# Weight splits of 1024 columns, and nine conditioning parts summed on VectorE, in a one-core diffusion step

## The chip, the cores and the metric

One core of a Trainium2 chip runs the whole program. The metric is the device time in microseconds from start to end of one execution, lower is better. The engines are TensorE (PE, with its weight loads PEld), VectorE (DVE), ScalarE (ACT), GpSimd (POOL) and SyncE (SP), whose queue issues the weight transfers. All work on the same on-chip memory, each through its own queue, in the order in which its instructions stand there.

## The reference

Two layers over 256 tokens (128 context, 128 latent) of width 2048, in float32: layer 0 mixes attention and a recurrent scan, layer 1 is a convolution module, and each is followed by a gated ffn of width 5504. Every norm is shifted, scaled and gated by vectors computed from two conditioning vectors; this is the part that the change touches:

```python
def adaln(cvec, w, b):
    return (jax.nn.silu(cvec) @ w + b)[:, None, :]
...
    sh1p, sc1p, g1p, sh2p, sc2p, g2p = jnp.split(adaln(c_ctx[None, :], w_ada[l], b_ada[l]), 6, axis=-1)
    sh1s, sc1s, g1s, sh2s, sc2s, g2s = jnp.split(adaln(c, w_ada[l], b_ada[l]), 6, axis=-1)
    hp = rmsnorm(xp, norm_g[l, 0]) * (1.0 + sc1p) + sh1p
...
def conv_ffn(h, w_up, w_dw, w_down):
    u = dwconv(h @ w_up, w_dw)
    gate, val = jnp.split(u, 2, axis=-1)
    return (jax.nn.silu(gate) * val) @ w_down
```

w_ada has 2 x 2048 x 12288 elements, and each is used for two vectors only. All other weights are used for all 256 tokens.

## The kernel before, in words

**The gemms.** Every large product goes through `gemm` (or `gemm_joint` for the first projection). Activations lie in memory as pairs of a rounded value and its remainder (`split`, `modulated`); weights are split in the same way, into `hi` and `lo`. For each slice of 128 rows of the inner dimension (a *k-step*) and each tile of 128 output columns, three matmuls of 256 tokens are issued (L251, L253, L254): hi with the value, hi with the remainder, lo with the value. A k-step of 512 weight columns is 12 matmuls. The ffn runs an up projection of the first 22 of 43 column blocks, a down projection of these, and then the same for the other 21.

**The weight stream.** `sub_iter` walks over all plans in a fixed order and gives one load of up to 1024 columns (512 KB) into a `raw` buffer, of which there are seven, then one conversion per k-step. `emit_sub` issues the load from SP, copies the columns to `hi` on ScalarE (L194), and subtracts on VectorE, or on GpSimd in the first conv gemm and for half of the second, to get `lo` (L196). The eight slots of `wbt` each hold one k-step. `next_sub` keeps the stream six k-steps ahead of TensorE.

**The conditioning.** `ada_order` lists 30 parts; the first ten are narrow (two or four blocks of 128 columns), the other 20 have 8 blocks, 1024 columns. `ada_pe` computes a part on TensorE: silu of the two vectors, padded to 32 columns, is the stationary operand, and w_ada streams past it as four matmul calls of 256 columns per 128 rows (L429). In the late parts a step is two raw loads and eight such calls; eight steps make a part. `ada_turn` transposes the result on VectorE, and `ada_gen` adds the bias and sets the part as done. Loads for w_ada take their buffers from the same seven as the weights, in the order of the code.

**What sets the order.** The code calls `ada_step` from the `fill` functions of the gemms: every sixth k-step in both ffns (`fill0`, `fill2`, after the sixteenth), every fourth in the conv gemm (`fill1`) and in the output projection. `ada_until` runs what is left where a part is needed: g2 ahead of the down projection, sh1 of layer 1 ahead of the conv module, g1 ahead of its second gemm, sh2 behind that gemm, ahead of the second ffn. Between the two conv gemms a depthwise convolution of 31 taps ends, on VectorE and, in late groups, on TensorE (L1608). The scheduler then orders each engine's instructions by the code's order and its own estimate of times; the raw buffers rotate.

## Time and profile before

| | |
|---|---|
| median of 3 runs | 2783.12 us (2778.12 to 2791.07) |
| the profiled execution | 2783.63 us, span 2781.1 us |
| mean granted TensorE clock | 0.977 |
| raw<-in_w_ada | 384 loads, 512 KB each, median 5.5 us to landing |
| matmul instructions L429 on w_ada | 3840 in 1920 calls, between 13.8 and 2215.0 us |

By time from the start of the span: the first projection, up to about 260 us, with the narrow parts beside it; the recurrent scan and attention up to about 750 us; the output projection; the first ffn from about 840 to 1640 us; the first conv gemm to 1890, the second from 1915 to 2009; the second ffn to the end.

A row of the windows gives a stretch in us, then busy us and number of instructions of PE, PEld, DVE, ACT and POOL, the granted clock, the busy share of the DMA engines and what they moved in GB/s. A row of groups gives line, engine, operation, what is written from what, count, busy us and mean length in ns, then the idle time before them and what ended it. Rows of the timeline and of the chain of waits begin with start and length in us. Matmuls overlap, so that time per matmul is read from a stretch and its count, not from its length.

### The profile page before, as it was taken

Reading aid. Unit: us, or ns where it says so; the run is one execution under the profiler, and the core shown is the slowest. Engines: PE = TensorE matmul, PEld = TensorE weight load, DVE = VectorE, ACT = ScalarE, POOL = GpSimd, SP = SyncE. Lnnn points to the kernel's source line nnn. Section 1 sums busy time; section 2 is a strip of 40 time slices with the busy share of each in tenths; the row PEclk is TensorE's granted clock in tenths of the full one; section 3 lists DMA queues with packets and bytes.
Section 4 is the critical chain, followed back from the end, with each engine's and each line's share of the span. In section 5 each row is a group of like instructions: output and inputs, shape, how many; then the busy total and the mean of one; then the engine's idle time right before and its main releaser. Section 6 shows DMA issues by size and latency. Waiting matters only on the chain.

```text
span 2781.1 us, 64420 instructions
## 1 busy us (share of the span) xinstructions
PE 2709.5 (97%) x25355; PEld 2496.1 (90%) x25355; DVE 1777.3 (64%) x3873; ACT 1404.9 (51%) x2866; POOL 321.7 (12%) x409
## 2 busy tenths in 40 slices
PE   6999998999999999999999999999999999999998
PEld 5899995767999999999999988988999999999998
DVE  3568757666568656546656558997476665566665
ACT  4336644545446545434555455447565554455554
POOL 2000011111100000000000017765300000000000
PEclk9999999989899999999999999999999999999999
DMA  9996657656276887788788767883568865565563
GB/s 295 327 281 215 178 154 258 219 165 220 94 232 208 267 257 250 259 263 252 250 267 261 261 204 257 289 251 107 182 207 254 268 189 189 185 189 183 174 199 113
DMA packets 446991, 616.83 MB, mean 222 GB/s; under 512 B 33461, under 2 KB 317464, under 8 KB 446048
## 3 DMA queue, kind: packets, MB, share of 16 engines
q1 hardware_dynamic: 442288, 600.83, 68.4%
q0 software_dynamic: 3040, 6.57, 0.7%
q10 hardware_dynamic: 1360, 5.33, 0.5%
q8 instruction: 198, 3.24, 0.5%
q14 instruction: 105, 0.86, 0.1%
HBM read 604.75 MB, written 7.86 MB: 220 GB/s over the span
## 4 chain that ended last, share of the span: by engine, by line
PE 94%; DMA 2%; DVE 2%; ACT 1%; issue 0%; SPq 0%; DVEq 0%; ACTq 0%
PE mm L251 24%; PE mm L254 23%; PE mm L253 23%; PE ada L429 7%; DMA raw<-in_w_ada 2%; PE mm L1050 2%; PE mm L303 1%; PE mm L304 1%; PE mm L305 1%; PE mm L1608 1%; PE mm L288 1%; PE mm L1083 1%; DVE hbt L550 1%; PE mm L290 1%; DMA raw<-in_w_in 1%; PE mm L291 1%
## 5 line engine op out<-in xcount | busy, mean ns | idle before, releaser
L194 ACT ACTIVATE wbt<-raw 128x512 fp32r<-128x512 f32 (+2 forms) x1560 | 945.4, 612 | 1073.7 <-PE mm L253 803.9
L196 DVE TENSOR_TENSOR wbt<-raw,wbt 128x512 fp32r<-128x512 f32 (+2 forms) x1384 | 922.6, 672 | 732.0 <-ACT wbt L194 708.1
L251 PE MATMUL mm<-hbt,wbt 128*128 128x256 f32 x3888 | 1102.6, 285 | 5.5 <-ACT hbt L548 3.5
L253 PE MATMUL mm<-hbt,wbt 128*128 128x256 f32 x3888 | 1089.6, 281 | 4.3 <-DVE hbt L550 4.3
L254 PE MATMUL mm<-hbt,wbt 128*128 128x256 f32 x3888 | 1088.6, 280 | 0.0
L251 PEld LDWEIGHTS mm<-hbt,wbt 128*128 128x128 f32 x3888 | 732.2, 189 | 44.6 <-ACT wbt L194 20.2
L253 PEld LDWEIGHTS mm<-hbt,wbt 128*128 128x128 f32 x3888 | 731.9, 188 | 9.1 <-DVE hbt L550 7.1
L254 PEld LDWEIGHTS mm<-hbt,wbt 128*128 128x128 f32 x3888 | 734.5, 189 | 1.0 <-issue 0.4
L251 PE MATMUL mm<-u,wbt 128*128 128x256 f32 x1344 | 378.5, 282 | 0.0
L253 PE MATMUL mm<-u,wbt 128*128 128x256 f32 x1344 | 375.0, 279 | 0.0
L254 PE MATMUL mm<-u,wbt 128*128 128x256 f32 x1344 | 375.0, 279 | 0.0
L196 POOL TENSOR_TENSOR wbt<-raw,wbt 128x512 fp32r<-128x512 f32 (+1 forms) x176 | 215.4, 1234 | 961.9 <-ACT wbt L194 946.1
L251 PEld LDWEIGHTS mm<-u,wbt 128*128 128x128 f32 x1344 | 252.2, 188 | 8.6 <-ACT wbt L194 7.4
L429 PE MATMUL ada<-raw,silu_c 128*32 128x256 f32 (+2 forms) x3840 | 238.3, 347 | 20.9 <-DVE ht L545 8.4
L254 PEld LDWEIGHTS mm<-u,wbt 128*128 128x128 f32 x1344 | 252.7, 188 | 0.0
L253 PEld LDWEIGHTS mm<-u,wbt 128*128 128x128 f32 x1344 | 251.4, 187 | 0.0
L429 PEld LDWEIGHTS ada<-raw,silu_c 128*32 128x32 f32 x3840 | 99.3, 110 | 95.2 <-issue 18.9
L1615 DVE SCALAR_TENSOR_TENSOR cu<-mm,vec,cu 128x256 f32<-128x256 f32 x428 | 174.6, 471 | 2.8 <-ACT cu L1599 1.2
L1504 DVE SCALAR_TENSOR_TENSOR cv<-mm,vec,cv 128x254 f32<-128x254 f32 x344 | 148.1, 474 | 14.1 <-ACT cv L1499 14.0
L303 PE MATMUL mm<-hbt,wbt 128*128 128x256 f32 x304 | 90.4, 298 | 0.4 <-ACT hbt L548 0.3
L304 PE MATMUL mm<-hbt,wbt 128*128 128x256 f32 x304 | 85.7, 282 | 0.0
L305 PE MATMUL mm<-hbt,wbt 128*128 128x256 f32 x304 | 85.0, 280 | 0.0
(443 smaller groups left out, 2772.4 us busy)
## 6 DMA issues: line engine op xcount, KB each, us to landing
raw<-in_w_ada SPq DMA_DIRECT2D x384, 512.0 KB, 5.5
raw<-in_w_up SPq DMA_DIRECT2D x688, 256.0 KB, 3.7
raw<-in_w_down SPq DMA_DIRECT2D x168, 512.0 KB, 4.6
raw<-in_w_pw SPq DMA_DIRECT2D x128, 256.0 KB, 5.0
raw<-in_w_in SPq DMA_DIRECT2D x128, 192.0 KB, 5.8
raw<-in_w_in SPq DMA_DIRECT2D x48, 512.0 KB, 3.9
raw<-in_w_out SPq DMA_DIRECT2D x32, 512.0 KB, 4.5
raw<-in_w_pw SPq DMA_DIRECT2D x32, 512.0 KB, 4.5
```

The costliest lines, as they stand in the source:

```text
L194: act.activation(w[:, 0, 0:n], src, AF.Copy)
L196: pl.lo(pl.count).tensor_tensor(out=w[:, 1, 0:n], in0=src, in1=w[:, 0, 0:n].bitcast(F32), op=ALU.subtract)
L251: pe.matmul(ps, lhsT=hi, rhs=r[:, 0:TT], start=(ki == 0 and (nl > 0 or j % 2 == 0)), stop=False, skip_group_check=True)
L253: pe.matmul(ps, lhsT=hi, rhs=r[:, TT:2 * TT], start=False, stop=False, skip_group_check=True)
L254: pe.matmul(ps, lhsT=lo, rhs=r[:, 0:TT], start=False, stop=(ki == nk - 1), skip_group_check=True)
L303: pe.matmul(ps, lhsT=hi, rhs=r[:, 0:TT], start=(i == 0), stop=False, skip_group_check=True)
L304: pe.matmul(ps, lhsT=hi, rhs=r[:, TT:2 * TT], start=False, stop=False, skip_group_check=True)
L305: pe.matmul(ps, lhsT=lo, rhs=r[:, 0:TT], start=False, stop=(i == len(rw) - 1), skip_group_check=True)
L429: pe.matmul(ps[32 * j:32 * j + 32, 0:nb * 32], lhsT=silu_c[:, kt, :], rhs=rv[:, j], start=(kt == 0), stop=(kt == KT - 1))
L1050: pe.matmul(dst_[h][:, s * TT:(s + 1) * TT], lhsT=src[pr, s], rhs=kr[pr, s].rearrange("p a t -> p (a t)"), start=True, stop=True)
L1504: dve.scalar_tensor_tensor(out=o[:, :, a_], in0=v2(ps)[:, :, b_], scalar=w(k, ct), in1=o[:, :, a_], op0=ALU.mult, op1=ALU.add)
L1615: dve.scalar_tensor_tensor(out=o, in0=pads[a](k), scalar=V("w_dw", k * KT + ct), in1=o, op0=ALU.mult, op1=ALU.add)
```

## The change

It has three parts. The weight split works on a whole load: `emit_load` issues the load, one ScalarE copy and one subtract of up to 1024 columns, and `wbt` has four slots of 1024 columns, each given back when all its k-steps were used. Nine conditioning parts (`AS_VEC`) are no longer multiplied on TensorE: `ada_vec` multiplies each load of w_ada by the silu value of its row (a scalar per partition) and adds it to an accumulator `av`, once per vector, on VectorE; what is left, a sum over 128 partitions, is made by eight matmul calls with a selector `sel`, four per vector. And the fills call `ada_step` every second k-step in both ffns, in the first one only until part (1, g1, 0) is done. A part in `ada_vec` has 38 steps, where one of `ada_pe` had ten.

```diff
-    WB = 8
-    LA = WB - 2
+    WB = 4
+    LA = 6
...
-        wbt[0] = wbp.tile([P, WB, 2, 512], F32R, tag="wb", name="wbt")
+        wbt[0] = wbp.tile([P, WB, 2, 1024], F32R, tag="wb", name="wbt")
...
+        if len(ends) >= WB and ends[-WB] > free[0]:
             return False
...
+        w = wbt[0][:, len(ends) % WB]
+        act.activation(w[:, 0, 0:na * n], v, AF.Copy)
+        pl.count += 1
+        pl.lo(pl.count).tensor_tensor(out=w[:, 1, 0:na * n], in0=v, in1=w[:, 0, 0:na * n].bitcast(F32),
+                                      op=ALU.subtract)
+        subs.extend(w[:, :, a * n:(a + 1) * n] for a in range(na))
+        ends.append(len(subs))
...
+    AS_VEC = [(l, nm, i) for l, nm in ((0, "g2"), (1, "sc1"), (1, "sh1"), (1, "g2")) for i in range(2)] + [(1, "g1", 0)]
...
+    def ada_vec(l, nm, b0, nb):
...
+        nxt = load(0)
+        yield
+        for kt in range(KT):
+            raw, nxt = nxt, (load(kt + 1) if kt < KT - 1 else None)
+            for s in range(2):
+                sc = silu_c[:, kt, s:s + 1]
+                if kt == 0:
+                    dve.tensor_scalar(out=av[:, s], in0=raw, scalar1=sc, scalar2=None, op0=ALU.mult)
+                else:
+                    dve.scalar_tensor_tensor(out=av[:, s], in0=raw, scalar=sc, in1=av[:, s], op0=ALU.mult, op1=ALU.add)
+                yield
+        for _ in range(3):
+            yield
+        ps = psa.tile([P, 256], F32, tag="ada", name="ada")
+        for s in range(2):
+            rv = av[:, s].rearrange("p (b j c) -> p j b c", j=4, c=32)
+            for j in range(4):
+                pe.matmul(ps[32 * j:32 * j + 32, 0:nb * 32], lhsT=sel[:, s], rhs=rv[:, j], start=(s == 0), stop=(s == 1))
+        yield
+        return ada_turn(ps, nb)
...
-            tr = yield from ada_pe(l, nm, b0, nb, 2 if l or nm == "g2" else 1)
+            if (l, nm, part) in AS_VEC:
+                tr = yield from ada_vec(l, nm, b0, nb)
+            else:
+                tr = yield from ada_pe(l, nm, b0, nb, 2 if l else 1)
...
-                if cnt[0] % 6 == 0 and cnt[0] > 16:
+                if cnt[0] % 2 == 0 and cnt[0] > 16 and (1, "g1", 0) not in ada_done:
                     ada_step()
...
-                if cnt[0] % 6 == 0 and cnt[0] > 16:
+                if cnt[0] % 2 == 0 and cnt[0] > 16:
                     ada_step()
```

The parts that stay on TensorE after the first ffn are the second of g1 and all of sc2 and sh2 of layer 1. Their steps still run in `fill1` and, what is left, at the `ada_until` calls behind it. On the SP queue, from the end of the first conv gemm to the second ffn (`in_w_pw` are the conv weights, 128x2x512 those of the second gemm; `in_w_up` those of the ffn), there stood before:

```order
L566 DMA raw<-in_w_pw 128x4x128 x2
L410 DMA raw<-in_w_ada 128x1024 x2
L566 DMA raw<-in_w_pw 128x4x128 x6
L566 DMA raw<-in_w_pw 128x2x512 x32
L569 DMA raw<-in_w_up 128x2x256 x24
L410 DMA raw<-in_w_ada 128x1024 x2
```

and in the changed kernel:

```order
L603 DMA raw<-in_w_pw 128x2x512
L412 DMA raw<-in_w_ada 128x1024 x2
L603 DMA raw<-in_w_pw 128x2x512 x2
L412 DMA raw<-in_w_ada 128x1024 x10
L603 DMA raw<-in_w_pw 128x2x512 x29
L606 DMA raw<-in_w_up 128x2x256 x4
L412 DMA raw<-in_w_ada 128x1024 x30
L606 DMA raw<-in_w_up 128x2x256 x20
L444 DMA raw<-in_w_ada 128x1024
```

Ten loads of w_ada now stand ahead of the fourth load of the second conv gemm, and 30 behind the first two loads (four k-steps) of the ffn. On TensorE, at the end of the second conv gemm (L267 to L269 are its last matmuls, `ones` and `dg` the norm's), there stood before:

```order
L267 MATMUL mm<-hbt,wbt 128x256
L268 MATMUL mm<-hbt,wbt 128x256
L269 MATMUL mm<-hbt,wbt 128x256
L491 MATMUL mm<-ones,acc 128x2
L491 MATMUL mm<-ones,sq 128x2
L491 MATMUL mm<-ones,acc 128x2
L491 MATMUL mm<-ones,sq 128x2
L506 MATMUL mm<-dg,ones 128x256
L251 MATMUL mm<-hbt,wbt 128x256 x2
```

and in the changed kernel:

```order
L270 MATMUL mm<-hbt,wbt 128x256
L431 MATMUL ada<-raw,silu_c 32x256 x28
L528 MATMUL mm<-ones,acc 128x2
L528 MATMUL mm<-ones,sq 128x2
L528 MATMUL mm<-ones,acc 128x2
L528 MATMUL mm<-ones,sq 128x2
L431 MATMUL ada<-raw,silu_c 32x256 x8
L543 MATMUL mm<-dg,ones 128x256
L431 MATMUL ada<-raw,silu_c 32x256 x24
L252 MATMUL mm<-hbt,wbt 128x256 x2
L431 MATMUL ada<-raw,silu_c 32x256 x4
```

The calls on 16 loads of w_ada stand between the conv gemm and the third matmul of the ffn, and those on 14 more (not shown) among its first four k-steps and ahead of the fifth. On VectorE, in the second up projection of the first ffn (L196 and L194 are conversions, L1504 and L1544 the ffn's taps, L1512, L1519, L1552 and L1559 its products and splits, L456 the new sums), a piece of the queue before:

```order
L1504 SCALAR_TENSOR_TENSOR cv<-mm,vec,cv 128x2x127 x2
L196 TENSOR_TENSOR wbt<-raw,wbt 128x512
L1504 SCALAR_TENSOR_TENSOR cv<-mm,vec,cv 128x2x127 x4
L196 TENSOR_TENSOR wbt<-raw,wbt 128x512
L1504 SCALAR_TENSOR_TENSOR cv<-mm,vec,cv 128x2x127
L196 TENSOR_TENSOR wbt<-raw,wbt 128x512
L1504 SCALAR_TENSOR_TENSOR cv<-mm,vec,cv 128x2x127
L1512 TENSOR_TENSOR cv<-cv 128x256
L196 TENSOR_TENSOR wbt<-raw,wbt 128x512
```

and in the changed kernel:

```order
L1544 SCALAR_TENSOR_TENSOR cv<-mm,vec,cv 128x2x127 x2
L456 SCALAR_TENSOR_TENSOR av<-raw,silu_c,av 128x1024 x2
L194 TENSOR_TENSOR wbt<-raw,wbt 128x1024
L1544 SCALAR_TENSOR_TENSOR cv<-mm,vec,cv 128x2x127 x2
L194 TENSOR_TENSOR wbt<-raw,wbt 128x1024
L456 SCALAR_TENSOR_TENSOR av<-raw,silu_c,av 128x1024 x2
L194 TENSOR_TENSOR wbt<-raw,wbt 128x1024
L1552 TENSOR_TENSOR cv<-cv 128x256 x2
L194 TENSOR_TENSOR wbt<-raw,wbt 128x1024 x2
```

A pair of sums of 1024 columns now stands between conversions of 1024, and the conversions behind it on the queue come after it.

More of the change, by code (lines that the diff above doesn't have):

```diff
@@ L154, in __init__ @@
             self.count = 0
-    stream = {"slot": 0, "stop": None}
+    stream = {"stop": None}
     def sub_iter():
@@ L164, in sub_iter, with emit_load @@
                     na = min(1024 // g['n'], len(kts) - i)
-                    yield ("load", pl, g, kts[i], na)
-                    for a in range(na):
-                        yield ("conv", pl, g, kts[i], a)
+                    yield pl, g, kts[i], na
                     i += na
     subs = []
+    ends = []
+    used = [0]
+    free = [0]
     stream_it = [None]
-    def emit_sub():
+    def emit_load():
         if stream['stop'] is not None and len(subs) >= stream['stop']:
+            return False
+        if len(ends) >= WB and ends[-WB] > free[0]:
             return False
@@ L177, in emit_sub, with next_sub @@
             stream_it[0] = sub_iter()
-        while True:
-            ev = next(stream_it[0], None)
-            if ev is None:
-                return False
-            kind, pl, g, kt, a = ev
-            n = g["n"]
-            if kind == "load":
-                raw = rawp.tile([P, 1024], F32, tag="raw", name="raw")
-                v = raw[:, 0:a * n]
-                pl.view(sp, v, g, kt, a)
-                stream["raw"] = v
-                continue
-            raw = stream["raw"]
-            w = wbt[0][:, stream["slot"] % WB]
-            stream["slot"] += 1
-            src = raw[:, a * n:(a + 1) * n]
-            act.activation(w[:, 0, 0:n], src, AF.Copy)
-            pl.count += 1
-            pl.lo(pl.count).tensor_tensor(out=w[:, 1, 0:n], in0=src, in1=w[:, 0, 0:n].bitcast(F32), op=ALU.subtract)
-            subs.append(w)
-            return True
+        ev = next(stream_it[0], None)
+        if ev is None:
+            return False
+        pl, g, kt, na = ev
+        n = g["n"]
+        raw = rawp.tile([P, 1024], F32, tag="raw", name="raw")
+        v = raw[:, 0:na * n]
+        pl.view(sp, v, g, kt, na)
+        w = wbt[0][:, len(ends) % WB]
[5 more added lines that the diff above has]
+        ends.append(len(subs))
+        return True
     def prefetch(n=LA):
         while len(subs) < used[0] + n:
-            if not emit_sub():
+            if not emit_load():
                 break
-    used = [0]
-    def next_sub(la=LA):
+    def next_sub(la=LA, held=False):
+        if not held:
+            free[0] = used[0]
         prefetch(1 + la)
@@ L432, in ada_pe, with load @@
         return ada_turn(ps, nb)
+    def ada_vec(l, nm, b0, nb):
+        nw = nb * P
+        c0 = SEG[nm] * D + b0 * P
+        av = nrm_[0].tile([P, 2, 1024], F32, tag="av", name="av", bufs=1)
+        def load(kt):
+            raw = rawp.tile([P, 1024], F32, tag="raw", name="raw")
+            sp.dma_start(out=raw, in_=A["w_ada"][l, kt * P:(kt + 1) * P, c0:c0 + nw])
+            return raw
+        nxt = load(0)
[18 more added lines that the diff above has]
+        return ada_turn(ps, nb)
     def ada_turn(ps, nb):
@@ L1429, in tile_step @@
         dve.memset(silu_c, 0.0)
+        dve.memset(sel, 0.0)
+        for s in range(2):
+            dve.memset(sel[:, s, s:s + 1], 1.0)
         nrm_[0] = nrm0_scope.enter_context(scoped("nrm0", 2, "right"))
```

5 lines of the change are left out of this document (3 added, 2 removed).

## The prediction

> **What bounds the kernel now.** I read the page first, for the busy shares and the chain that ended last.
>
> ```profile
> span 2781.1 us, 64420 instructions
> PE 2709.5 (97%) x25355; PEld 2496.1 (90%) x25355; DVE 1777.3 (64%) x3873; ACT 1404.9 (51%) x2866; POOL 321.7 (12%) x409
> ...
> PE 94%; DMA 2%; DVE 2%; ACT 1%; issue 0%; SPq 0%; DVEq 0%; ACTq 0%
> ```
>
> TensorE holds 94% of the chain, so TensorE time removed in a dense stretch is time gained. Next, windows: one in the first ffn, with conditioning work, and one in the second, behind it (busy us, with instructions in brackets, for PE, PEld, DVE, ACT, POOL; then granted clock, DMA share, GB/s).
>
> ```profile
> 980.00:1050.00 70.00, 70.00 (x632) 65.69 (x631) 43.20 (x81) 36.37 (x69) 0.00 (x0) 1.00 0.79 251
> 2450.00:2520.00 70.00, 70.00 (x597) 70.00 (x595) 46.32 (x86) 39.70 (x74) 0.00 (x0) 1.00 0.62 189
> ```
>
> TensorE never pauses in either. Without conditioning work 597 matmuls take 70 us, 0.1173 us each; a k-step (512 weight columns, 12 matmuls) takes 1.41 us. VectorE is busy for 43 to 46 of 70 us: it has some 25 us to give, no more. The chain of waits shows what a conditioning step on TensorE costs (start, length):
>
> ```profile
> 998.73 1.00 PE ada L429 x16
> ...
> 1008.41 1.00 PE ada L429 x16
> ```
>
> One such step (two loads, eight matmul calls, each two instructions) comes every six k-steps, and the spacing is 9.68 us. The six k-steps are 72 x 0.1173 = 8.44 us, so a step costs **1.24 us** of TensorE, and a part of eight steps 9.9 us.
>
> **The change, part by part.** The sum is made against the profiled execution: 2783.6 us, of which the span is 2781.1; the median of the three runs is 2783.1, so they are one.
>
> *TensorE work removed.* By the order of the two programs, the matmul calls on w_ada fall from 1920 to 1344, and the rest moves. Scan and output projection go from 432 to 384, the first ffn from 528 to 0, the second from 128 to 0; the conv stage goes from 192 to 200, and 120 new ones stand between the second conv gemm and the second ffn. The dense stages thus lose 48 + 528 + 128 - 8 = 696 calls, 87 steps: **-107.9 us**. Each of nine parts gets eight calls with the selector in return, in the same form (32 rows by 256 columns), 72 calls or nine steps: **+11.2 us**.
>
> *The 120 calls at the boundary.* Before, the gap is short (PE timeline: start, length, idle before).
>
> ```profile
> 2008.58 0.28 PE L269 MATMUL mm<-hbt,wbt 128*128 128x256 f32 x1
> 2010.72 0.35 PE L491 MATMUL mm<-ones,acc 128*128 128x2 f32 x2 [1.86 <-DVE acc L480]
> ...
> 2015.13 0.80 PE L251 MATMUL mm<-hbt,wbt 128*128 128x256 f32 x2 [1.17 <-ACT hbt L548]
> ...
> 2023.05 0.28 PE L251 MATMUL mm<-hbt,wbt 128*128 128x256 f32 x1
> ```
>
> From the last conv matmul (2008.6) to the fifth k-step of the ffn (2023.1) pass 14.5 us. In the changed program the SP queue holds weights for four k-steps of the ffn, then 30 loads of w_ada, then the weights for the fifth. There are seven raw buffers, so 7 of the 30 are in place when TensorE arrives and 23 stream behind it, each waiting for the one seven earlier to be used. How fast they stream is bounded by the busiest windows:
>
> ```profile
> 70.00:140.00 70.00, 69.62 (x853) 58.76 (x852) 41.75 (x112) 26.78 (x61) 0.00 (x0) 1.00 1.03 328
> 140.00:210.00 70.00, 69.59 (x732) 63.05 (x732) 42.69 (x107) 26.92 (x60) 0.00 (x0) 1.00 0.93 274
> 440.00:450.00 10.00, 10.00 (x83) 6.59 (x82) 1.43 (x4) 3.20 (x13) 0.20 (x2) 0.88 1.02 386
> ```
>
> A load of 0.524 MB takes 1.60 us at 328 GB/s, 1.36 at 386, 1.91 at 274. The raw tile's summary and the page give a landing:
>
> ```profile
> DMA to landing us min/median/max: 2.6/4.4/10.4
> ...
> raw<-in_w_ada SPq DMA_DIRECT2D x384, 512.0 KB, 5.5
> ```
>
> First landing 0.5 + 4.4 us behind the last conv matmul, 22 more at 1.60 (35.2), the fifth k-step's weights 1.6, their ScalarE copy 1.1 (0.631 + 512 x (0.631 - 0.398)/256, from L194's 512 and 256 columns in the fence after next): 42.8 us against 14.5, **+28 us**, between +23 (1.36) and +35 (1.91). I take 328 GB/s because it held for 70 us. The 15 steps' own TensorE time lies inside this wait.
>
> *The end of the first conv gemm.* 48 calls (12 loads) move in among the taps:
>
> ```profile
> 1893.32 10.92 PE mm L1608 x42
> ...
> 1900.00:1910.00 10.00, 10.00 (x61) 9.04 (x59) 4.50 (x10) 5.52 (x15) 0.00 (x0) 1.00 0.01 2
> ```
>
> TensorE is on the chain there, but DMA is idle. 96 instructions at 1.00/16 us are 6 us if nothing hides them, and 0 if the tap chain waits elsewhere; 12 loads in a row could make it 10. I take **+5 us**, near the 6.
>
> *VectorE.* Prices, from a stretch where it works without a pause (start, length), then groups: mean ns of one behind the bar, or min/median/max ns behind the colon:
>
> ```profile
> 1016.26 0.68 DVE L196 TENSOR_TENSOR wbt<-raw,wbt 128x512 fp32r<-128x512 f32 x1
> 1016.86 1.64 DVE L1504 SCALAR_TENSOR_TENSOR cv<-mm,vec,cv 128x254 f32<-128x254 f32 x4
> 1018.42 0.68 DVE L196 TENSOR_TENSOR wbt<-raw,wbt 128x512 fp32r<-128x512 f32 x1
> ...
> 1020.40 0.75 DVE L1512 TENSOR_TENSOR cv<-cv 128x256 f32<-128x256 f32 x2
> ...
> L1504 DVE SCALAR_TENSOR_TENSOR cv<-mm,vec,cv 128x254 f32<-128x254 f32 x344 | 148.1, 474 | 14.1 <-ACT cv L1499 14.0
> L1512 DVE TENSOR_TENSOR cv<-cv 128x256 f32<-128x256 f32 x86 | 35.0, 415 | 0.0
> L630 DVE SCALAR_TENSOR_TENSOR x<-mm,adaT,x 128x128 f32<-128x128 f32 x224 | 61.6, 342 | 18.4 <-PE mm L269 15.3 <-PE mm L254 3.1
> ...
> L194 ACT ACTIVATE wbt<-raw x1560: 398/631/672, 25.9 to 2755.4; 128x512 fp32r<-128x512 f32 x169, 128x384 fp32r<-128x384 f32 x16, 128x256 fp32r<-128x256 f32 x8, 128x448 fp32r<-128x448 f32 x2
> L196 DVE TENSOR_TENSOR wbt<-raw,wbt x1384: 412/691/1389, 26.5 to 2756.1; 128x512 fp32r<-128x512 f32 x172, 128x384 fp32r<-128x384 f32 x17, 128x256 fp32r<-128x256 f32 x5, 128x448 fp32r<-128x448 f32 x4
> ...
> L196 POOL TENSOR_TENSOR wbt<-raw,wbt 128x512 fp32r<-128x512 f32 (+1 forms) x176 | 215.4, 1234 | 961.9 <-ACT wbt L194 946.1
> ```
>
> Back to back, a 512-column subtract takes 0.60 us from start to start (1016.26 to 1016.86), though its own length is 0.68. Four taps take 1.56 (0.39 each), and two 256-column ops 0.75 with the last at 0.415, so 0.335 apart. The slope is (0.60 - 0.335)/256 us per column, and **a 1024-column op comes to 1.13 us**. The trace has no such op, and no summing one of that width; I price both so. Isolated, by length, it would be 0.691 + 512 x (0.691 - 0.412)/256 = 1.25 us, since 412 is the row of 256 columns.
>
> Per load of w_ada VectorE does two sums, in four k-steps (two fills each), beside two conversions of 1024. In an up projection the group's taps and products add (8 x 0.39 + 4 x 0.335)/4 = 1.12: together 4 x 1.13 + 1.12 = **5.64 us, against 5.63 us of TensorE**. In a down projection the residual adds 8 x 0.342 over 22 k-steps, 0.50 in four: 5.02. So the up halves with sums (about 102 of the 144 loads) run VectorE exactly full; the coarser conversions, which save 0.07 of each 1.20 us, are what makes it fit. At isolated lengths, evictions at their row means, it would be 4 x 1.25 + (8 x 0.474 + 4 x 0.415)/4 = 6.36, 0.73 us too much, 74 us over 102 loads. A gain has no source, since TensorE is full, so the bounds are 0 and +74. I take **+12 us**: an engine that is late works back to back, which puts it near the lower end, but the sums wait for their loads too (first rival). If a load is late, the conversions and taps queued behind that sum wait with it, and TensorE waits for those once its six converted k-steps are used.
>
> [...]
>
> *Weight slots of 1024.* Four slots of two k-steps hold what eight held. A slot comes free only when both its k-steps are done, so TensorE has six converted k-steps ahead instead of seven. Dense windows wait for nothing, so I put it at 0; the third rival is its price. ScalarE makes half as many copies, each 1.10 us in 2.81; GpSimd's conversions in the conv gemm, two of 1.234 us per two k-steps before, become one, no longer than both, so neither can become the bound: 0. On the SP queue, w_ada loads now stand singly between weight loads; three loads in four k-steps are 1.57 MB in 5.63 us, 279 GB/s, less than the 328 that held for 70 us: 0 beyond the landings below.
>
> Sum: 2783.6 - 107.9 + 11.2 + 28 + 5 + 12 = **2732 us**.
>
> **The rivals.**
>
> *The sums wait for the raw ring (slower).* A w_ada load may be issued only when the conversion seven raw tiles earlier is done, and that conversion stands on the same VectorE queue, in the median 6.1 us of work ahead of the sum (counted in the changed order at the prices above). Landing at 4.4 us leaves 17 us of waits over the 144 loads; 6 us makes 81, 7 us makes 165. VectorE can absorb some 83 us (the down halves 36 x 0.6, and the twelve k-steps of each part without a sum, 27 x 2.27). So it decides from about 6.5 us, and at 7 us the kernel is 2732 - 12 + 82 = **2802 us**. For it: 5.5 us for w_ada loads, 10.4 at most. Against it: those went out in pairs, the second behind the first.
>
> *VectorE pays full lengths.* Every op holds it for its own length: 2732 - 12 + 74 = **2794 us**, no measurable change. For it: the isolated ops of the dense windows; against it: the 0.60 us spacing.
>
> *The coarser slots show.* Each of some 26 up groups with sums brings a burst of 4.5 us of taps; if the shorter lead costs one k-step per group, 26 x 1.41 = 37 us: **2769 us**. For it: the slack falls by one k-step just where VectorE is full. Against it: six k-steps are 8.4 us, longer than the burst.
>
> **How the numbers follow.** The forecast, with its own range 2708 to 2768 (all low bounds: 2783.6 - 96.7 + 23; high: boundary 35, taps 10, VectorE 35, half its bound), has 0.72. The raw ring has 0.09, full lengths 0.10 (mostly within the bound, a part above), the coarser slots 0.09. The range goes from 2708 to 2794, where the 74 us of VectorE's upper bound end. Half a per cent, 14 us, is about what a measurement of this kernel can tell from no change: faster 0.72, same 0.15, slower 0.13.
>
> **What would show it.** Right: in the first ffn a window of 70 us with about 597 matmuls and hardly any on w_ada, TensorE at 70 of 70, VectorE at 65 or more; about 43 us between the last conv matmul and the fifth k-step of the second ffn, with DMA at 300 GB/s or more; sums of 1024 columns at 1.13 to 1.24 us. Wrong: weight loads on TensorE waiting for VectorE conversions in the ffns, sums waiting for w_ada landings above 6 us, or a boundary that is short because the scheduler's order hides it.

## The result and the profile after

The changed kernel takes **2710.7 us** in the median of four runs (2700.8 to 2725.8), the kernel before 2781.7 in four runs beside it: ratio 0.9744, 95% interval 0.9692 to 0.9797, faster. Six more runs, in the experiments, have a median of 2706.1 (ratio 0.9739, 0.9715 to 0.9764). The forecast was 2732 with a range from 2708 to 2794: the direction was right, the number was 21 to 26 us too high, and the first median lies in the range by 2.7 us, that of the six later runs 2 us below it.

Runs of one kernel differ by their mean granted clock: 29 runs of the kernel before at 0.979 to 0.981 have a mean of 2778.6 us, and 17 runs below 0.979 take 8 us more in the mean, up to 17. Where a few us matter, runs at 0.979 to 0.981 are compared below; they are called *runs at full clock*.

The page of the changed kernel, its busy shares and the chain that ended last:

```profile
span 2705.6 us, 60522 instructions
PE 2615.6 (97%) x24347; PEld 2443.4 (90%) x24347; DVE 2020.5 (75%) x3468; ACT 1258.5 (47%) x2074; POOL 298.7 (11%) x313
...
PE 84%; DVE 7%; DMA 6%; ACT 1%; issue 1%; SPq 0%; POOL 0%; DVEq 0%; ACTq 0%; POOLq 0%
```

TensorE is still the bound, but it holds 84% of the chain instead of 94%: VectorE (7% instead of 2%) and DMA (6% instead of 2%) have taken the rest. Windows of the changed kernel, columns as before; the first and the fifth are the two stretches shown of the kernel before, the second lies in the last up half of the first ffn, the third at the boundary ahead of the second ffn:

```profile
980.00:1050.00 70.00, 70.00 (x595) 68.91 (x594) 65.20 (x83) 34.54 (x51) 0.00 (x0) 1.00 0.83 261
1400.00:1470.00 70.00, 70.00 (x597) 70.00 (x596) 69.80 (x87) 34.30 (x51) 0.00 (x0) 1.00 0.84 264
1940.00:1980.00 40.00, 31.93 (x309) 15.83 (x307) 13.36 (x49) 7.34 (x21) 0.00 (x0) 0.77 0.94 340
2240.00:2310.00 70.00, 70.00 (x620) 70.00 (x619) 35.80 (x42) 26.94 (x27) 0.00 (x0) 1.00 0.61 195
2450.00:2520.00 70.00, 70.00 (x620) 70.00 (x620) 44.63 (x62) 35.29 (x50) 0.00 (x0) 1.00 0.64 195
```

The first two show what the prediction asked for: in the first ffn VectorE is busy for 65 to 70 of 70 us, and TensorE still does 597 matmuls in 70 us. The last two rows hold what the prediction had no place for: behind the last conditioning work, where the change touches nothing but the slots, 620 matmuls fit into 70 us, where the kernel before had 597, at the same granted clock of 1.00.

To see where the time went I read from both traces when each stage's first weight matmul starts (us, difference to the kernel before; positive is longer). The last two columns belong to experiments below. What is left of the scan runs beside the first half of the output projection.

```
stage                          before   changed    slots only   sums only (512)
first projections               357.8      +7.4       +5.3        +2.5
scan and attention, 1           327.3     -13.7      -12.3        -1.3
output proj., 1st half           63.0      -2.0       +4.8        -1.3
output proj., 2nd half           57.1      -3.6       +0.5        -1.5
first ffn                       816.1     -60.1       +6.6       -65.4
first conv gemm                 258.7      +4.3       -1.1        +0.1
second conv gemm                 98.9      +9.8       +1.2        +9.9
second ffn, first 4 k-steps       7.9     +15.0       -0.2       +15.1
rest of its first up half       263.0     -15.4       +0.3       -15.8
rest of the second ffn          481.9     -18.0        0.0         0.0
```

Most of the scan's -13.7 goes, by an estimate, with the clock of one execution. Windows of the kernel before and of the changed one in the scan (stretch, PE busy and count, granted clock, DMA share, GB/s):

```profile
550.00:560.00 10.00, 10.00 (x190) 0.76 0.64 215
560.00:570.00 10.00, 10.00 (x103) 0.50 0.03 9
570.00:580.00 10.00, 10.00 (x120) 0.72 0.28 65
```

```profile
550.00:560.00 10.00, 10.00 (x146) 1.00 0.46 132
560.00:570.00 10.00, 10.00 (x195) 1.00 0.46 170
570.00:580.00 10.00, 9.50 (x166) 1.00 0.50 155
```

In these 30 us the granted clock of the kernel before is 0.24, 0.50 and 0.28 below 1.00; taken as lost time that is 10.2 of the 30 us, an estimate from these rows. The profiled execution of the changed kernel had 1.00 there. The kernel with slots only, at 1.00 too, has -12.3 in the table; the one with sums only, at 0.84, 0.50 and 0.64, has -1.3. Both executions have a mean clock of 0.977, so the other one lost its share elsewhere; over runs at full clock such a difference should drop out. The rows of the first stages are no better than that: the kernel with one added call told below, the same program as before up to the second ffn, has +3.7 us in the first projections and -8.3 in the scan in its one trace.

### The profile page after: what moved, and what is told of

The parts are those of the page before. It is cut to its first block, busy times and chain, and to the rows that moved or that the text cites. A ratio compares the mean times of both kernels' runs of the same rounds, so it can differ in the third digit from the quotient of the medians.

```text
span 2705.6 us, 60522 instructions
## 1 busy us (share of the span) xinstructions
PE 2615.6 (97%) x24347; PEld 2443.4 (90%) x24347; DVE 2020.5 (75%) x3468; ACT 1258.5 (47%) x2074; POOL 298.7 (11%) x313
## 4 chain that ended last, share of the span: by engine, by line
PE 84%; DVE 7%; DMA 6%; ACT 1%; issue 1%; SPq 0%; POOL 0%; DVEq 0%; ACTq 0%; POOLq 0%
PE mm L255 22%; PE mm L252 22%; PE mm L254 22%; PE ada L431 4%; DVE cu L1655 3%; DMA raw<-in_w_ada 2%; DMA raw<-in_w_in 2%; PE mm L1087 1%; DVE wbt L194 1%; DMA raw<-in_w_up 1%; PE mm L304 1%; PE mm L306 1%; PE mm L305 1%; PE mm L1648 1%; PE mm L1120 1%
## 5 line engine op out<-in xcount | busy, mean ns | idle before, releaser
L192 ACT ACTIVATE wbt<-raw 128x1024 fp32r<-128x1024 f32 (+3 forms) x768 | 793.7, 1037 | 1035.4 <-PE mm L254 696.8
L252 PE MATMUL mm<-hbt,wbt 128*128 128x256 f32 x3888 | 1086.5, 282 | 6.0 <-ACT hbt L585 2.3
L254 PE MATMUL mm<-hbt,wbt 128*128 128x256 f32 x3888 | 1081.5, 280 | 2.7 <-DVE hbt L587 2.7
L194 DVE TENSOR_TENSOR wbt<-raw,wbt 128x1024 fp32r<-128x1024 f32 (+1 forms) x688 | 812.6, 1188 | 357.7 <-ACT wbt L192 345.5
L255 PE MATMUL mm<-hbt,wbt 128*128 128x256 f32 x3888 | 1064.2, 280 | 3.5 <-DVE wbt L194 3.3
L254 PE MATMUL mm<-u,wbt 128*128 128x256 f32 x1344 | 371.0, 278 | 0.0
L252 PE MATMUL mm<-u,wbt 128*128 128x256 f32 x1344 | 370.9, 278 | 0.0
L255 PE MATMUL mm<-u,wbt 128*128 128x256 f32 x1344 | 365.7, 278 | 0.0
L456 DVE SCALAR_TENSOR_TENSOR av<-raw,silu_c,av 128x1024 f32<-128x1024 f32 x270 | 337.2, 1278 | 29.6 <-DMA raw<-in_w_ada 29.5
L194 POOL TENSOR_TENSOR wbt<-raw,wbt 128x1024 fp32r<-128x1024 f32 x80 | 193.5, 2427 | 909.8 <-DMA raw<-in_w_pw 800.2
L431 PE MATMUL ada<-raw,silu_c 128*32 128x256 f32 (+2 forms) x2688 | 166.0, 337 | 31.3 <-DMA raw<-in_w_ada 15.6
L1544 DVE SCALAR_TENSOR_TENSOR cv<-mm,vec,cv 128x254 f32<-128x254 f32 x344 | 147.3, 474 | 11.8 <-ACT cv L1539 11.8
L431 PEld LDWEIGHTS ada<-raw,silu_c 128*32 128x32 f32 x2688 | 70.3, 112 | 91.7 <-issue 26.2
L304 PE MATMUL mm<-hbt,wbt 128*128 128x256 f32 x304 | 91.7, 302 | 1.9 <-DVE qkv L311 1.0
L1539 ACT ACTIVATE cv<-mm,vec 128x256 f32<-128x256 f32 x172 | 72.0, 474 | 45.9 <-PE mm L255 45.8
```

Of the source, the lines that this page charges most:

```text
L192: act.activation(w[:, 0, 0:na * n], v, AF.Copy)
L194: pl.lo(pl.count).tensor_tensor(out=w[:, 1, 0:na * n], in0=v, in1=w[:, 0, 0:na * n].bitcast(F32), op=ALU.subtract)
L252: pe.matmul(ps, lhsT=hi, rhs=r[:, 0:TT], start=(ki == 0 and (nl > 0 or j % 2 == 0)), stop=False, skip_group_check=True)
L254: pe.matmul(ps, lhsT=hi, rhs=r[:, TT:2 * TT], start=False, stop=False, skip_group_check=True)
L255: pe.matmul(ps, lhsT=lo, rhs=r[:, 0:TT], start=False, stop=(ki == nk - 1), skip_group_check=True)
L304: pe.matmul(ps, lhsT=hi, rhs=r[:, 0:TT], start=(i == 0), stop=False, skip_group_check=True)
```

## The experiments

Twelve runs tell the parts of the sum apart; their times are in one table, in the order in which they are told. The last column is the mean of the runs at full clock, with their number; for the changed kernel two runs of the first series and one of the second stand by themselves.

```
kernel                         runs  median   ratio [95%]               full clock
kernel before                                                           2778.6 (29)
changed, first four runs        4    2710.7   0.9744 [0.9692, 0.9797]   2700.8, 2725.8
changed, again                  6    2706.1   0.9739 [0.9715, 0.9764]   2705.6 (3), 2723.0
slots only                      9    2793.9   1.0052 [1.0032, 1.0071]   2789.9 (5)
sums only, 512                  4    2721.8   0.9786 [0.9766, 0.9805]   2718.9 (2)
no burst                        5    2727.9   0.9814 [0.9789, 0.9839]   2726.5 (4)
before + one call               4    2758.5   0.9925 [0.9910, 0.9940]   2758.4 (4)
sums, 512, call at 2 mod 3      4    2697.9   0.9706 [0.9692, 0.9721]   2697.7 (4)
sums, 512, call at 0 mod 3      4    2718.4   0.9779 [0.9762, 0.9795]   2717.2 (2)
spread                          4    2724.4   0.9806 [0.9787, 0.9824]   2721.6 (1)
calls in both ffns              4    2700.3   0.9685 [0.9645, 0.9724]   2684.7 (1)
sums twice as fast             10    2798.1   1.0067 [1.0037, 1.0097]   2791.0 (2)
before, seven slots            10    2774.7   0.9965 [0.9946, 0.9983]   2778.4 (5)
changed + one call              4    2729.3   0.9790 [0.9752, 0.9829]   2723.1 (2)
```

### The changed kernel again

No edit.

> The changed kernel once more, unchanged. In its profiled run the 4218 matmuls behind the last selector run (from 2207 us) came every 0.1133 us, nearly everything ahead of them every 0.1178 us, at a granted clock of 1.00 in both. Theory 'the pace belongs to the program': the same again, 0.113 us from the last selector run to the end, time within 3 us of 2708. Rival 'the pace is drawn anew in every execution, at an interruption': the second ffn comes out at 0.118 us over some or all of its length, in which case the time is up to 19 us longer (4218 x 0.0045), about 2727; the four times of this kernel, from 2701 to 2726, would be such draws.

The profiled run took 2706.9 us and repeated the pattern to the matmul: 620 per 70 us from the last selector run to the end. Five of the six runs lie between 2704.1 and 2708.8, one at 2723.0. So the pace repeats in two traces, and a free draw in every execution falls. That the runs of 2723.0 and, in the first series, 2725.8, both at full clock, ran their second ffn at the slow pace would fit, but no trace of them exists. The 2705.6 us used below is the mean of three runs of this series without the one of 2723.0; all six runs of the changed kernel at full clock, from both series, have a mean of 2711.1.

### Only the slots, and only the sums

```diff
-    AS_VEC = [(l, nm, i) for l, nm in ((0, "g2"), (1, "sc1"), (1, "sh1"), (1, "g2")) for i in range(2)] + [(1, "g1", 0)]
+    AS_VEC = []
...
-                if cnt[0] % 2 == 0 and cnt[0] > 16 and (1, "g1", 0) not in ada_done:
+                if cnt[0] % 6 == 0 and cnt[0] > 16:
```

(and the same sixth k-step in the second ffn, parts of g2 in steps of two loads)

> Only the weight slots of 1024 columns; all parts of w_ada are summed on TensorE again, one step every six k-steps, as before. Theory (the prediction's 0 for this part): no change that can be measured, 2783 within 10 us, VectorE's busy time some 60 us less than before (0.07 of each 1.2 us). Rival 'the coarser slots show': TensorE has one converted k-step less in hand and waits once per up group, some 26 groups x 1.41 us, up to 2820. A second rival from the stages of the changed kernel, where the scan is 14 us shorter and the joint projection 7 us longer, though little of the sums lies there: those come from the slots, which would give about 2775.

The other half is the kernel before with `ada_vec`, `sel` and the fills of the changed kernel, and its own `emit_sub` with eight slots of 512.

> Only the nine parts summed on VectorE; the weights are converted 512 columns at a time into eight slots, as before. Theory (the prediction: the coarser conversions are what makes the sums fit): VectorE has 2 x 1.13 + 4 x 0.60 + 1.12 = 5.78 us of work per four k-steps in an up half, against 5.63 of TensorE, so it becomes the bound there, some 15 us over 102 loads more than the changed kernel: about 2725, TensorE waiting for VectorE conversions in the up halves. Rival 'VectorE had room': the same as the changed kernel, 2710, and the slots do nothing. By the lengths of isolated ops (2 x 1.28 + 4 x 0.69 + 1.36 = 6.68) it would be 2710 + 100 = 2810 at most.

The slots alone cost time: 2789.9 against 2778.6 at full clock, 11 us. The stage table does not have it once per up group; the rival's mechanism falls, its sign stands. Where the 11 us lie is shown in part only. The gap between the first ffn and the conv gemm is 10.1 to 11.5 us in all six traces with wide slots and 6.2 to 6.9 in the eight with 512. The +5.3 in the first projections hardly stands out from the +3.7 that the program before has in another execution, and the +4.8 in the first half of the output projection is in none of the other traces with wide slots. The sums alone make 2718.9, **59.7 us** less than before: they are the whole gain, and the changed kernel is 13 us below that only through its second ffn (0.0 against -18.0 in the last row of the table).

The theory behind the second expectation, that the coarser conversions are what makes the sums fit, falls as well. Two windows of the kernel with sums and 512 columns, columns as before:

```profile
970.00:1040.00 70.00, 70.00 (x597) 70.00 (x596) 68.23 (x109) 39.35 (x74) 0.00 (x0) 1.00 0.85 263
1300.00:1370.00 70.00, 70.00 (x597) 70.00 (x596) 69.48 (x111) 38.27 (x72) 0.00 (x0) 1.00 0.83 263
```

VectorE is as full, and in both stretches TensorE doesn't wait for it. In the first ffn this kernel is 5 us faster than the changed one, 3.4 of them in the gap at its end. VectorE's sums there waited 24.6 us in all for loads of w_ada in the changed kernel, and 2.8 us in this one. The row of the sums in the groups between 840 and 1580 us, first of the changed kernel, then of this one (count | busy us, mean ns | idle time ahead of them):

```profile
L456 DVE SCALAR_TENSOR_TENSOR av<-raw,silu_c,av 128x1024 f32<-128x1024 f32 x204 | 254.5, 1278 | 24.7 <-DMA raw<-in_w_ada 24.6
```

```profile
L456 DVE SCALAR_TENSOR_TENSOR av<-raw,silu_c,av 128x1024 f32<-128x1024 f32 x204 | 260.1, 1288 | 2.9 <-DMA raw<-in_w_ada 2.8
```

### The burst at the boundary

```diff
-                    if cnt[0] % 4 == 0 and (1, "sh2") not in ada_done and cnt[0] > 16:
+                    if cnt[0] % 2 == 0 and (1, "sh2") not in ada_done and cnt[0] > 16:
```

> The changed kernel, but inside the first conv gemm a step of conditioning every second k-step instead of every fourth, so that the 120 calls at the boundary and the 48 at the end of that gemm are done inside it. Theory 'the burst costs what its loads take': the second conv gemm and the first four k-steps of the second ffn, 24.8 us longer in the changed kernel than before, are as short as before, and the 21 steps cost 21 x 1.24 = 26 us of TensorE inside the dense gemm instead, less some 5 at the end of that gemm: about 4 us faster than the changed kernel, 2706. Rival 'the burst hides the steps': the boundary saves little, and the steps cost their 26 us in full, 2720 to 2730. Rival 'VectorE is the bound in the first conv gemm': the steps are hidden there and the kernel gains up to 25 us, 2686.

Against the profile of before, the second conv gemm is +0.5 us and the first k-steps of the second ffn 0.0, instead of +9.8 and +15.0: the burst did put 24.8 us there. The first conv gemm is +23.1 instead of +4.3: the 21 steps cost 18.8 us in it, less than the 26 expected. By stages this kernel is 6 us ahead at the boundary, as the theory had it. Yet it took 2726.5 us, 21 more than the changed kernel. Its second ffn runs at 0.1178 us per matmul from the last selector run to the end, which is 18 of them; with the 6 gained at the boundary some 9 us stay unexplained (3 between the two profiled executions). The two kernels have the same instructions there, two selector runs with 20 matmuls between them. In the changed kernel the stretch ahead of the first run is slow, and the second one makes it quick; here that stretch is slow too, the *first* run makes it quick, and the second slow again.

### Two paces

That pointed to a rule, and I tabulated it over the traces: for every run of conditioning matmuls among the weight matmuls behind 800 us, how many matmuls lie between it and the run ahead of it, and the pace in front of it and behind it. From the slow pace a short run (up to eight instructions) leads to the quick one where that number is 2 modulo 3, in 35 of 39 cases over all traces, against 6 of 42 at 1 and 0 of 31 at 0. The slow pace is 353.3 ns per three matmuls, the quick one 340. Three experiments could break the rule, each with one added call of two instructions whose result nothing reads:

```diff
+    def mark(at):
+        if due and due[0] == at:
+            due.pop(0)
+            ps = psa.tile([P, 256], F32, tag="ada", name="ada")
+            pe.matmul(ps[0:32, 0:256], lhsT=silu_c[:, 0, :], rhs=silu_c.rearrange("p k c -> p (k c)")[:, 0:256],
+                      start=True, stop=True)
...
+                    mark(0)
                     pe.matmul(ps, lhsT=hi, rhs=r[:, 0:TT], start=(ki == 0 and (nl > 0 or j % 2 == 0)), stop=False,
                               skip_group_check=True)
+                    mark(1)
                     pe.matmul(ps, lhsT=hi, rhs=r[:, TT:2 * TT], start=False, stop=False, skip_group_check=True)
+                    mark(2)
```

> The kernel before, with a single 32x256 matmul call (two instructions, its result read by nothing) put into the second ffn behind the last conditioning step, between the second and the third matmul of a triple, 134 matmuls behind that step. Theory 'TensorE keeps one of two paces from one interruption to the next, and an interruption turns the slow pace into the quick one where the number of matmuls since the one before is 2 modulo 3': 134 is 2 modulo 3, so the 4540 matmuls behind it come every 0.1133 us instead of 0.1178: 20 us less, less 0.75 us for the call itself, ratio 0.993, about 2759 where the kernel before takes 2779. Rival 'the quick pace comes from the sums on VectorE or the wide slots': nothing, 2780. Rival 'chance': either.

> The kernel with sums on VectorE and slots of 512 (its second ffn ran at 0.1178 us per matmul throughout), with one 32x256 matmul call behind the last selector run, 89 matmuls behind it (2 modulo 3). Theory of the two paces: quick from there to the end, 4040 matmuls x 0.0045 = 18 us less and 0.75 us more, about 2719 - 17 = 2702 in runs without a lowered clock. Rivals as in the run before it: 2720.

> The same as the kernel before it, the call one matmul later: 90 matmuls behind the last selector run (0 modulo 3). Theory of the two paces: slow to the end, 2720. Rival 'any short interruption draws the pace anew': as likely quick as slow. If this one is quick and the one before slow, the rule by modulo 3 falls.

All three came out as the rule says: 2758.4, 2697.7 and 2717.2 us at full clock, where 2759, 2702 and 2720 were expected. The timelines of the two kernels with sums, at the call (start, length); first 89 matmuls behind the last selector run, then 90:

```profile
2219.83 0.28 PE L265 MATMUL mm<-u,wbt 128*128 128x256 f32 x1
2219.95 0.28 PE L267 MATMUL mm<-u,wbt 128*128 128x256 f32 x1
2220.16 0.62 PE L241 MATMUL ada<-silu_c 128*32 128x256 f32 x2
2220.71 0.39 PE L262 MATMUL mm<-u,wbt 128*128 128x256 f32 x1
2220.93 0.28 PE L265 MATMUL mm<-u,wbt 128*128 128x256 f32 x1
2221.05 0.28 PE L267 MATMUL mm<-u,wbt 128*128 128x256 f32 x1
```

```profile
2225.49 0.28 PE L267 MATMUL mm<-u,wbt 128*128 128x256 f32 x1
2225.61 0.28 PE L262 MATMUL mm<-u,wbt 128*128 128x256 f32 x1
2225.82 0.62 PE L241 MATMUL ada<-silu_c 128*32 128x256 f32 x2
2226.37 0.39 PE L265 MATMUL mm<-u,wbt 128*128 128x256 f32 x1
2226.59 0.28 PE L267 MATMUL mm<-u,wbt 128*128 128x256 f32 x1
2226.71 0.28 PE L262 MATMUL mm<-u,wbt 128*128 128x256 f32 x1
```

The call itself looks alike in both. What follows does not. Windows 200 us later in the same two kernels and in the kernel before with its one call (stretch, PE busy and count, granted clock, DMA share, GB/s):

```profile
2450.00:2520.00 70.00, 70.00 (x620) 1.00 0.65 194
```

```profile
2450.00:2520.00 70.00, 70.00 (x597) 1.00 0.62 185
```

```profile
2450.00:2520.00 70.00, 70.00 (x620) 1.00 0.64 193
```

One added call in 64420 instructions makes the *kernel before* 20 us faster, without any sum on VectorE or wide slot.

### Spreading the burst

Sums and 512 slots, a step every third k-step in the first conv gemm, and:

```diff
-    AS_VEC = [(l, nm, i) for l, nm in ((0, "g2"), (1, "sc1"), (1, "sh1"), (1, "g2")) for i in range(2)] + [(1, "g1", 0)]
+    AS_VEC = [(l, nm, i) for l, nm in ((0, "g2"), (1, "sc1"), (1, "sh1"), (1, "g2")) for i in range(2)] + [(1, "g1", 0), (1, "sh2", 1)]
...
-                gemm(p_p2, lambda kt: hc[:, kt], residual(1, "g1", acc), tail=4)
+                def fill_p2():
+                    if (1, "sh2") not in ada_done:
+                        ada_step()
+                gemm(p_p2, lambda kt: hc[:, kt], residual(1, "g1", acc), fill_p2, tail=4)
```

> Sums on VectorE and slots of 512, and the steps of the boundary taken elsewhere: inside the first conv gemm a step every third k-step instead of every fourth, and the last part (second half of the second shift of layer 1) summed on VectorE during the second conv gemm. Theory: the second conv gemm and the boundary fall by the 25 us that the burst put on them, TensorE does 9 more steps in the first conv gemm (11 us) and one more selector run (1.2 us), the end of that gemm loses two steps: about 2719 - 13 = 2706 in runs without a lowered clock, the second ffn at the slow pace (916 and 36 matmuls between its last selector runs, 1 and 0 modulo 3). Rival 'VectorE has no room in the conv gemms': TensorE waits for conversions there, 2719 or more.

A miss: 2721.6 at full clock in its one such run, median 2724.4, no gain over 2718.9. The boundary is as short as before (+0.9 us), but the first conv gemm is +17.6 and the second +16.9. A window between the two conv gemms shows why:

```profile
1860.00:1900.00 40.00, 31.70 (x238) 30.84 (x239) 38.93 (x59) 24.51 (x50) 23.09 (x16) 0.88 0.48 146
```

VectorE is busy for 39 of 40 us and TensorE for 32 only: the scheduler drew the new sums ahead, among the work of the norm that the second conv gemm waits for. The rival is right that VectorE has no room there, but what TensorE lacks is mostly the norm's result, not conversions: in the stretch from 1590 to 1990 us its waits for conversions are 6.0 us, those for what the norm makes 15.2.

### The pace in the first ffn

Sums and 512 slots, with nine calls whose k-step and place in the triple were chosen behind each selector run (their operands are the weights and activations of the matmuls beside them):

```diff
+                at = {32: 2, 84: 2, 236: 2, 312: 2, 388: 2, 465: 2}.get(cnt[0])
+                if at is not None:
+                    due.append(at)
...
+                at = {30: 0, 101: 2, 184: 1}.get(cnt[0])
```

> Sums on VectorE, slots of 512, and nine single 32x256 matmul calls in the two ffns, each placed 2 modulo 3 matmuls behind the last selector run ahead of it (the first of each ffn behind the last pause at its start, whose place is not sure). Theory of the two paces: most of the first ffn and of the first up half of the second at 0.1133 us, the rest of the second too. First ffn: some 4300 matmuls x 0.0045 - 6 x 0.75 = 15 us; first up half of the second: 1650 x 0.0045 - 2 x 0.75 = 6 us; behind it 18 - 0.75 = 17 us as already seen: 2719 - 38 = 2681 in runs without a lowered clock. Rival 'VectorE holds the first ffn': its conversions and sums fill 65 to 69 of 70 us there already, so a quicker TensorE only waits for it, the first ffn gains nothing, 2696. Rival 'the rule holds only in the second ffn': the same 2696 by another cause (the pace there stays 0.1178 and there are no pauses).

The one run at full clock took 2684.7 us, within 4 of the 2681 expected; the median, 2700.3, is that of runs at a clock of 0.973 to 0.974. The trace doesn't bear the agreement out: the profiled executions of this kernel and of the one without calls, both at a clock of 0.974, took 2702.2 and 2726.4 us, a gain of 24 us where 38 were expected. In the first ffn five of the six calls turned the pace to quick; the sixth, the first of all, followed pauses and was lost. The first ffn gained 9.1 us on the kernel without calls, not 15. VectorE explains a part of the rest: TensorE pauses for 1.9 us at 1254 and for 0.5 to 0.7 at 1457, 1464 and 1470, and three of these four end a quick stretch. In the first up half of the second ffn the rule worked against the placing: there a selector run had already made the pace quick (32 matmuls, 2 modulo 3), and the call behind it made it slow; that stage gained nothing.

### How much VectorE has in hand

```diff
-                if cnt[0] % 2 == 0 and cnt[0] > 16 and (1, "g1", 0) not in ada_done:
+                if cnt[0] > 16 and (1, "g1", 0) not in ada_done:
```

> The changed kernel with a step of the sums every k-step of the first ffn instead of every second: the same sums, in half the length, and none in the rest of that ffn. By the spacings in the trace of the changed kernel (sum 1.20 us, conversion 1.14, taps and products 1.12 per four k-steps) VectorE has 2 x 1.20 + 1.14 + 0.56 = 4.10 us of work per two k-steps in an up half, against 2.83 of TensorE. Theory 'the six converted k-steps in hand cover what VectorE lacks, part by part': at the present rate the lack is 5.80 - 5.63 = 0.17 us per load, 2.7 us per part of 16 loads, under the 8.4 us in hand, so TensorE hardly waits; at double rate it is 1.27 us per load, 20 us per part, and TensorE waits for all of that but the 8.4 us and some 3 us made up between parts: 8 us or more in each of 5 to 6 parts, up to 100 us in all, 2750 to 2800. Rival 'VectorE has room that the spacings do not show': 2706, as the changed kernel.

2791.0 us at full clock, 85 us more than the changed kernel with the same sums, inside the expected range and near its upper end. A window of the first up half, and how long TensorE waited for conversions in the first ffn up to 1320 us, then in the changed kernel from 840 to 1580 us (engine and line, for what, us in total, times, longest):

```profile
970.00:1040.00 70.00, 57.39 (x441) 53.86 (x439) 66.83 (x82) 24.80 (x36) 0.00 (x0) 0.95 0.80 247
```

```profile
PE mm L255 <- DVE wbt L194: 52.2, 57, 2.5
```

```profile
PE mm L255 <- DVE wbt L194: 3.3, 4, 1.4
```

VectorE is no fuller than at the single rate (67 of 70 us), but now TensorE waits for its conversions. The rival falls, and with it the reading that a VectorE at 65 to 70 of 70 us must show on TensorE.

### One slot less

```diff
-    WB = 8
+    WB = 7
```

> The kernel before with seven weight slots of 512 columns instead of eight, and five sub-slots ahead instead of six, nothing else. In runs of equal clock the wide slots alone cost 11 us (2789.5 against 2778.5), in the joint projections (5), the second scan stage (5), and the gap between the first ffn and the conv gemm (5). Theory 'that is the price of having one converted k-step less in hand': this kernel shows it too, 2784 to 2790, in the same stages. Rival 'it is the price of the longer single operations (load 0.5 MB, copy 1.04 us and conversion 1.14 us before the first of two k-steps can start)': no difference here, 2779.

2778.4 at full clock against 2778.6: no difference (its median is lower because five of its ten runs had a clock above 0.981). The 11 us of the wide slots are not the price of a k-step less in hand. That they are the price of longer single operations follows only by exclusion and is not shown; wide slots in greater number were not tried.

### Ending the quick pace in the changed kernel

The call of the three kernels above, 224 matmuls behind the last selector run.

> The changed kernel with one 32x256 matmul call (two instructions, its result read by nothing) 224 matmuls behind its last selector run, which had set the quick pace. Theory 'an interruption ends the quick pace, and the pace behind the last selector run is what the prediction missed': slow from the call to the end, 4044 x 0.0045 = 18 us and 0.75 us for the call: 2705 + 19 = 2724 in runs without a lowered clock, which is also where the two long runs of the changed kernel at an undisturbed clock lie (2723.0 and 2725.8). Rival 'the stretch is quick for another reason (VectorE, ScalarE or the DMA are calmer there with wide slots)': 2706.

2723.1 us at full clock (two runs, 2719.6 and 2726.6), 17.5 more than the 2705.6 of the changed kernel. The trace changes pace at the call, from 0.1133 to 0.1178 us. So the last row of the stage table, -18.0, is the pace and nothing else.

## Why the prediction was right, and 21 us too high

Runs at full clock give -73.0 us for the change (2778.6 to 2705.6; -67.5 with all six runs of the changed kernel at full clock), the sum gave -51.7. That the first median fell into the range is close to luck: its lower end, 2708, should be 2709.9 by its own terms (2783.6 - 96.7 + 23), and nothing in it allowed for a quicker TensorE. Point by point:

- **TensorE work removed and added (-107.9 and +11.2): right.** Its place is the two ffns and the output projection. In the first ffn 66 steps less and six selector runs more made -74.4 by the prediction's 1.24 us. That price is a little high: the 597 of a window count the matmuls that overlap its ends, while from start to start a matmul takes 0.1178 us (353.3 ns per three), so that a step costs 9.68 - 72 x 0.1178 = 1.20 us and the whole sum holds 3 us too much gain. Measured are -65.4 with 512 slots and -60.1 with wide ones, with VectorE's waits and whatever the slots cost in them. In the first up half of the second ffn 14 steps net are -17.4; -15.4 measured.
- **The boundary (+28): right, measured +24.8.** The mechanism is in the trace. From the last conv matmul (1940.95) to the fifth k-step of the ffn (1980.50) pass 39.6 us where 42.8 were predicted; DMA moved 340 GB/s, not 328. The timeline of the changed kernel there (start, length, idle before):

```profile
1940.95 0.28 PE L270 MATMUL mm<-hbt,wbt 128*128 128x256 f32 x1
...
1954.88 1.08 PE L431 MATMUL ada<-raw,silu_c 128*32 128x256 f32 x8 [1.57 <-DMA raw<-in_w_ada]
...
1980.50 0.58 PE L252 MATMUL mm<-hbt,wbt 128*128 128x256 f32 x1 [1.60 <-ACT wbt L192]
```

- **The end of the first conv gemm (+5): within its bounds.** That gemm is +0.1 with 512 slots and +4.3 with wide ones, where the sum had 7.5 in it (+5, and one step and one selector run more at 1.24 each).
- **VectorE (+12): mechanism right, size too large.** The step that failed is "the up halves with sums (about 102 of the 144 loads) run VectorE exactly full", taken as a loss per load. The prices were near: back to back a conversion takes 1.13 us (1411.41 to 1412.54) and a sum 1.19 (1425.13 to 1426.32), where 1.13 was taken for both:

```profile
1411.41 1.21 DVE L194 TENSOR_TENSOR wbt<-raw,wbt 128x1024 fp32r<-128x1024 f32 x1
1412.54 2.48 DVE L456 SCALAR_TENSOR_TENSOR av<-raw,silu_c,av 128x1024 f32<-128x1024 f32 x2
...
1425.13 1.28 DVE L456 SCALAR_TENSOR_TENSOR av<-raw,silu_c,av 128x1024 f32<-128x1024 f32 x1
1426.32 0.87 DVE L1544 SCALAR_TENSOR_TENSOR cv<-mm,vec,cv 128x254 f32<-128x254 f32 x2
```

  That is 5.76 us of VectorE (2 x 1.19 + 2 x 1.13 + 1.12) in 5.63 of TensorE, so VectorE does fall behind, by 0.13 us per load. But a part is 16 loads, 2 us, and TensorE has six converted k-steps, 8.4 us, in hand; between two parts VectorE makes it up. The pauses of TensorE in the two up halves, from start to start, sum to 5.5 us in the changed kernel's trace and 1.1 in that of before; with sums and slots of 512 they are 1.1 too. The prediction had this allowance in its first rival ("VectorE can absorb some 83 us") and left it out of the term. The doubled rate shows the other side: where a part lacks more than the 8.4 us, TensorE waits.
- **Wide slots (0): wrong by a little, and their merit was wrong.** Alone they cost 11 us; beside the sums about 4 (2723.1 for the changed kernel at the slow pace, 2718.9 with 512 slots, two runs of each). "The coarser conversions are what makes it fit" is refuted by the kernel without them.
- **The missing term: -18 us.** The sum took 0.1173 us per matmul as TensorE's own pace and had no place for another. That is the larger part of the miss: without the quick pace the change makes 2723.1, 8.9 us below the forecast in us and 4 below it in the difference (-55.5 against -51.7). Even these 4 are luck in part: VectorE (by some 7), the boundary (3) and the end of the conv gemm (3) were priced too high, the wide slots and the price of a step the other way.

Of the rivals, *the sums wait for the raw ring* shows as far as its first step (29.5 us of waits for w_ada landings, 5.3 us in the median); VectorE absorbed most of them, and TensorE's pauses are the 5.5 us above. *VectorE pays full lengths* is refuted by the spacing: sums of 1.28 us start 1.19 us apart. *The coarser slots show* had the right sign and neither the place nor the size.

## What to carry to other kernels

When work is moved to an engine with little room, compare what it lacks per burst with what the bound engine has in hand, not the busy shares: the same sums made TensorE pause for some 4 us more at one rate, and made the kernel 85 us longer at twice that rate. Prefetched work that is left for a boundary is paid there in full by its transfers, 25 us here; moving it into a dense stage only trades them for 19 us of TensorE. And before a difference of a per cent is put down to a change, count the matmuls in a window that the change doesn't touch.

## What the hardware showed beyond that

TensorE has two steady paces in this kernel's dense stretches, 597 and 620 matmuls of 128x256 in 70 us, both at a granted clock of 1.00 and with PE and PEld busy for 70.00 of 70 us. A pace holds for thousands of matmuls (4218 in the changed kernel) until something interrupts the stream. Over all 14 traces, behind 800 us, where both the stretch ahead of a run of conditioning matmuls and the one behind it have a clear pace:

```
run of up to 8 instructions,     matmuls since the run ahead of it,    quick behind it
pace ahead of it                 modulo 3
slow                             2                                     35 of 39
slow                             1                                      6 of 42
slow                             0                                      0 of 31
quick                            any                                    0 of 33
longer runs                      any                                    0 of 585
```

Eight of the ten exceptions follow a run of 12 to 16 instructions. The counts move by a few with what is called a clear pace, and the kernels share most of their program, so the cases are not independent. The kernel before puts its runs, of 16 instructions, at the ends of k-steps, a multiple of 12 matmuls apart, and stays slow from 280 us on nearly without a break: of 15181 spacings over three such matmuls in its trace, up to 2700 us, 14700 lie between 345 and 362 ns and 194 between 330 and 345. What in the chip holds the pace, and why three, stays open: the rule is read from traces and was tested by the five kernels with added calls, no more.

The best version measured is the kernel with sums on VectorE, slots of 512 and one added call: 2697.9 us, ratio 0.9706 (0.9692 to 0.9721), ahead of the changed kernel's 0.9739 (0.9715 to 0.9764); the intervals overlap a little, the four runs (2696.4 to 2698.7) and the ten of the changed kernel (from 2700.8 up) do not. The one with calls in both ffns may be better still (2684.7 in its one run at full clock), but its interval, 0.9645 to 0.9724, does not show it.
